# Weight sums of a seven-product MLP: two of four made by adding transfers, and one copy placed ahead of a cast

## The chip, the cores and the metric

The kernel runs on one core of a Trainium2 chip. The metric is the device time of one execution in microseconds, as the median of several runs. The core's engines are TensorE (PE in the profile; its weight loads are PEld), VectorE (DVE), ScalarE (ACT), GpSimd (POOL) and SyncE (SP). Here SP only issues transfers, and POOL issues those transfers that add to what stands at their destination.

## The reference, cut to what matters

The kernel computes one layer of a diffusion backbone in float32 for 512 latent tokens of width 2048. After the two attention mixers comes the channel mixer, a gated MLP of 5632 hidden features, which is the part that the change touches:

```python
def _conv_ffn(h, w_up, conv_w, conv_b, w_down):
    g, u = jnp.split(h @ w_up, 2, axis=-1)
    T = g.shape[1]
    pad = CONV_W // 2
    gp = jnp.pad(g, ((0, 0), (pad, pad), (0, 0)))
    g = sum(gp[:, j:j + T] * conv_w[j] for j in range(CONV_W)) + conv_b
    return (jax.nn.silu(g) * u) @ w_down
...
        h2 = _modulate(_rmsnorm(x, norm2_w[l]), sh2, s2)
        x = x + g2 * _conv_ffn(h2, w_up[l], conv_w[l], conv_b[l], w_down[l])
    return _rmsnorm(x, final_w)
```

## The kernel before, in words

The hidden features are cut into 44 tiles of 128 (`ft` 0 to 43). Each has a gate half `g` and an `u` half, each the sum over the 2048 input features of weight times activation. Tiles 0 to 2 are multiplied plainly (jobs `("n", ...)` and `("u", ...)`). For each of the tiles 3 to 43 the two halves of the outputs (g, u) times the two halves of the input features form a 2 by 2 block of weights, 128x1024 each: `w11`, `w12`, `w21`, `w22`. Against the 2 by 2 block of the activations (two halves of the features, two halves `h0`, `h1` of the tokens) this is a product of two 2 by 2 matrices, done with seven block products instead of eight. They are jobs `("p", ft, k)`, k from 0 to 6. Product 0 takes `w11`, product 1 `w21`, product 4 the sum `t3`, product 5 `w22`, and products 2, 3 and 6 take other sums of weights. For that, sums of the four weight blocks are made for every tile (`weight_sum`), and sums of activation blocks once, ahead of the tiles (`sums`). In the kernel before, all four weight sums of a tile are subtractions on DVE, 128x1024 each: L1534 makes `ws` 1 = w12 - w11 in the job of product 6 of the tile before; L1537 makes `ws` 2 = w22 - `ws` 1 in the job of product 0; L1540 turns w12 into t3 = w22 - w12 in product 1's; L1544 makes `ws` 2 = w21 - `ws` 2 in product 2's.

Every weight operand is split in a high and a low part: ACT casts it to `wh` (`cast`, L1575) and DVE subtracts that from it, giving `wl` (`low`, L1583). `wh` and `wl` have three buffers each, so a cast waits until PE has finished with the operand three jobs back.

PE collects products in three kinds of PSUM tile, `y`, `z` and `x`. Products 0, 2, 4 and 6 add to one and the same `y` tile, and between them ACT copies its state away (`kept`, L1517, to one of two buffers `m`); product 2 may not start before the copy that follows product 0 is done. DVE puts the copies together (`put_together`, L1522 and L1523), the gate goes through ACT (L1491), DVE (L1495, L1497) and ACT (L1502), is multiplied with `u` (`multiply`, L1506) and is split in `ah` and `al` for the down projection.

The down projection of a group of four tiles is eight jobs `("d", c, dp)`, of 24 matmuls each, that lie between the products of the next group. `DOWN_AFTER` puts them into the tiles with ft % 4 = 1 (after products 0, 1, 3, 4, 6) and ft % 4 = 2 (after 0, 2, 3). The tiles with ft % 4 = 3 and 0 have none. ACT scales the outputs of a down block into two buffers `xs` (L1778) and POOL adds them to `x1_d` in HBM with an adding transfer (L1779).

What sets the order: PE, ACT, DVE and SP get their instructions as the code writes them (`manual_schedule`); those of POOL are placed by the framework's scheduler. In each job `strassen(i)` writes the product i on PE, then the weight sum, then the cast for job i+2, then `after(jobs[i - 1])` (the copies and sums that follow the job before), then the low part for job i+2. Each engine works its queue strictly in order.

Loads are issued by SP out of two rings of three buffers of 512 KB: `wr` for w11, the plain tiles' and the down projection's weights, `rb` for the other three blocks of a tile. `Ring.pump` issues a load as soon as the ring's next buffer has no use left (`used`), at that place of SP's queue.

Of the kernel before, what the change touches and what calls it, by code (L numbers as in the profile page):

```python
# [9 lines left out]
F32 = mybir.dt.float32  # L10
# [3 lines left out]
ALU = mybir.AluOpType  # L14
# [3 lines left out]
P = 128  # L18
# [9 lines left out]
NFT = DFF // P  # L28
# [178 lines left out]
def layer_kernel(ctx: ExitStack, tc: tile.TileContext, small, rope, c_row, cc_row, x_t, ctx_t, ada, ada_k,  # L207
                 w_g0, w_f, w_v, w_uqn, w_uqr, w_ukv, w_o, w_up0, w_up, w_dn, out_t):
    nc = tc.nc
    pe, ve, sc, gp = nc.tensor, nc.vector, nc.scalar, nc.gpsimd  # L210
# [6 lines left out]
    n = [0]  # L217

    def nm(s):
        n[0] += 1  # L220
        return f"{s}{n[0]}"
# [39 lines left out]


    sm = ctx.enter_context(tc.tile_pool(name="sm", bufs=1))
    sm.tile([P, 88], F32, name="edge")
# [20 lines left out]
    modx = cst.tile([P, 96], F32, name="modx")  # L285
# [122 lines left out]
    for i, j, view, d in spread:  # L408
        t, o = (cb, ccb)[i], slice(j * 512, j * 512 + 512)
# [357 lines left out]
    for half in range(2):  # L767
# [18 lines left out]
        for t in order:  # L786
            hl = []
# [594 lines left out]
    class Ring:  # L1382

# [62 lines left out]
    def sums(j):  # L1446

        a, c = hf[j], hf[j + 8]
        d1, d2, d3, d4 = c[:, h1], a[:, h0], a[:, h1], c[:, h0]
        b1_, b2_ = db[:, j:j + 1], modx[:, 56 + j:57 + j]  # L1450

        def first():
            t1[j] = a2k(F32R, apb)
            for t in (t3, t2, t4):
                t[j] = spare.pop(0) if spare else b2k(F32R)
            ve.tensor_tensor(d1, c[:, h1], a[:, h1], op=ALU.add)
# [45 lines left out]
        sc.activation(t, t, AF.Silu)  # L1502
        return t

    def multiply(t, u):
        ve.tensor_tensor(t, t, u, op=ALU.mult)  # L1506
# [13 lines left out]
    def put_together(dst, a, b):  # L1520

        ve.tensor_tensor(b, a, b, op=ALU.add)  # L1522
        ve.tensor_tensor(dst, b[:, h0], b[:, h1], op=ALU.add)  # L1523

    def weight_sum(ft, i):

        if ft >= NFT:
            return
        ra, rb = mem["ra"], mem["rb"]
        w12, w21, w22 = (rb.tiles.get((k, ft)) for k in ("w12", "w21", "w22"))  # L1530
        if i in (1, 2):
            sums_[ft, i] = mem["mm"].tile([P, 1024], F32, tag="ws", name=nm("ws"), bufs=2)
        if i == 1:
            ve.tensor_tensor(sums_[ft, 1], w12, ra.tiles["w11", ft], op=ALU.subtract)  # L1534
            ra.used(("w11", ft))
        elif i == 2:
            ve.tensor_tensor(sums_[ft, 2], w22, sums_[ft, 1], op=ALU.subtract)  # L1537
            rb.used(("w22", ft))
        elif i == 3:
            ve.tensor_tensor(w12, w22, w12, op=ALU.subtract)  # L1540
            rb.used(("w12", ft))
            rb.used(("w22", ft))
        else:
            ve.tensor_tensor(sums_[ft, 2], w21, sums_[ft, 2], op=ALU.subtract)  # L1544
            rb.used(("w21", ft))

    def operand(job):

        ra = mem["ra"]
        if job[0] != "p":  # L1550
            return ra.tiles[job], lambda: ra.used(job)
        ft, k = job[1:]
# [4 lines left out]
        key = ({1: "w21", 4: "w12", 5: "w22"}[k], ft)  # L1557
        return mem["rb"].tiles[key], lambda: mem["rb"].used(key)

    def kept_parts(i):  # L1560
# [158 lines left out]
    def third_tile(i):  # L1719
        b, w = jobs[i][1], weights(i)  # L1720
        if b == 0:
            live["s"] = [b_tile(g_, 2) for g_ in "yz"]
        for j in range(8):
            kt = (b // 2) * 8 + j
            classical(live["s"][b % 2], kt, w[j], kt == 0, kt == KT - 1)
        if b == 1:

            mem["hp"].release()
            mem["hr"].release()
            mem["mm"] = tc.alloc_tile_pool(name="mm", bufs=1, side="right", reuse_waits="tile")  # L1730
            mem["rb"] = Ring(mem["mm"], "rb", 3, items_b)
        cast(i + 2)
        if b < 2:
            t = gate_in(b, live["n"][2 * b])
            fill(2 + b)
            low(i + 2)
            silu(convolve(b, live["n"][2 * b], t))
            fill(2 + b)
            hl = multiply(t, live["n"][2 * b + 1])
            fill(1 - b)  # L1740
            acts[b] = finish(t, hl)
        else:
            fill(3)
            low(i + 2)
            weight_sum(3, b - 1)
            fill(5)


# [21 lines left out]
    def after(job):  # L1770

        if job == ("u", 3):
            live[2] = {"g": live["s"][0], "u": live["s"][1], "t": gate_in(2, live["s"][0])}
        elif job[0] == "d":
            for d, po in enumerate(live["po"]):
                dt = job[2] * 2 + d
                x = mem["mm"].tile([P, T], F32, tag="xs", name=nm("xs"), bufs=XS)
                sc.mul(x, po, modx[:, 80 + dt:81 + dt])  # L1778
                gp.dma_start(x1_d[dt], x, accum_op=ALU.add)  # L1779
        if job[0] != "p":  # L1780
            return
        ft, k = job[1:]
        v, f = live[ft], live.get(ft - 1)
        if k == 0:
            v["m1"] = kept(v["y"])
        elif k == 2:
            v["u2"] = kept(v["y"])
            if f:
                silu(convolve(ft - 1, f["g"], f["t"]))
        elif k == 3:  # L1790
            if f:
                acts[ft - 1] = multiply(f["t"], f["u"])
            v["g"] = mem["mm"].tile([P, T], F32, tag="g", name=nm("g"), bufs=1)
            put_together(v["g"][:, h0], v["x"], v["m1"])
            v["m5"] = kept(v["z"])
        elif k == 4:
            if f:
                finish(f["t"], acts[ft - 1])
            v["u"] = mem["mm"].tile([P, T], F32, tag="u", name=nm("u"), bufs=1)
            put_together(v["u"][:, h1], v["y"], v["m5"])  # L1800
        elif k == 5:
            put_together(v["u"][:, h0], v["z"], v["u2"])
        elif k == 6:
            sc.copy(v["g"][:, h1], v["y"][:, h1])
            ve.tensor_tensor(v["g"][:, h1], v["y"][:, h0], v["g"][:, h1], op=ALU.add)
            v["t"] = gate_in(ft, v["g"])

    def strassen(i):
        job = jobs[i]
        if job[0] == "p":  # L1810
            ft, k = job[1:]
            product(ft, k, weights(i))
            if k in (1, 2) or (k == 0 and ft > 3):
                weight_sum(ft, k + 2)
# [12 lines left out]
        low(i + 2)  # L1827


# [209 lines left out]
```

## Time and profile before

| | |
|---|---|
| runs shown, us | 2363.7, 2368.77, 2368.84 (median 2368.77) |
| profiled execution, us | 2363.86 |
| its span, first to last instruction, us | 2362.0 |
| PE busy over the span | 2307.2 us, 98% |
| DVE busy over the span | 1738.1 us, 74% |
| ACT busy over the span | 1141.0 us, 48% |
| POOL busy over the span | 243.6 us, 10% |
| mean granted TensorE clock | 0.994 |
| tiles 3 to 43 with their seven products | from 1052 to about 2300 us of the span |

A busy time counts the modelled length of the instructions. A matmul's end is modelled, and matmuls overlap, so PE can show as busy while it loses time: the distance between the starts of two products tells more than the busy share. In a row of the timeline the bracket at the end is how long the engine sat idle before that row, and what ended it. In rows of waits the numbers are the sum of the idle time, the number of waits, and the longest.

### The profile page before, as it was taken

What the parts mean: (1) busy time and instruction counts of PE and PEld (TensorE: products, weight loads), DVE (VectorE), ACT (ScalarE), POOL (GpSimd) and SP (SyncE); (2) the same over time, 40 slices, a digit from 0 to 9 for tenths busy, and PEclk for the clock granted to TensorE, in tenths of its full rate; (3) what the DMA queues carried; (4) which work ended last, traced back from release to release, by engine and by line L of the source; (5) the groups of instructions that cost most, each with busy time, mean ns of one, the idle gap of its engine ahead of it and who ended that gap; (6) DMA issues with size and microseconds to landing.
All of it is one profiled execution on the core that took longest, in us unless ns stands there. A gap on an engine that the chain in (4) does not pass through costs nothing.

```text
span 2362.0 us, 32374 instructions
## 1 busy us (share of the span) xinstructions
PE 2307.2 (98%) x12526; PEld 1969.4 (83%) x12526; DVE 1738.1 (74%) x2280; ACT 1141.0 (48%) x1736; POOL 243.6 (10%) x258
## 2 busy tenths in 40 slices
PE   6999999999999999999999999999999999999998
PEld 4788888888788888898888888888888888888887
DVE  7998786599977766597585858585857576767767
ACT  5331221477867622364454445454545454544546
POOL 0000000100033213000101010101010101011110
PEclk7999999999999999999999999999999999999999
DMA  9968888635311188334637474646464656455573
GB/s 344 341 256 311 324 341 316 197 119 139 135 60 41 50 329 291 98 106 126 160 105 169 110 169 109 155 128 152 125 141 128 143 141 144 122 156 125 144 188 107
DMA packets 130492, 404.25 MB, mean 171 GB/s; under 512 B 14337, under 2 KB 25089, under 8 KB 119841
## 3 DMA queue, kind: packets, MB, share of 16 engines
q1 hardware_dynamic: 103858, 351.64, 44.8%
q0 software_dynamic: 25328, 49.49, 12.1%
q8 instruction: 98, 1.61, 0.3%
q10 hardware_dynamic: 1152, 1.05, 0.1%
q14 instruction: 56, 0.46, 0.1%
HBM read 332.45 MB, written 69.67 MB: 170 GB/s over the span
## 4 chain that ended last, share of the span: by engine, by line
PE 77%; issue 14%; DVE 4%; ACT 2%; POOL 1%; DMA 1%; SPq 0%; DVEq 0%; POOLq 0%; ACTq 0%
PE y L1758 10%; PE b L258 9%; PE b L259 9%; PE b L260 9%; PE z L1758 5%; PE y L1760 5%; PE s L258 4%; PE s L259 4%; PE s L260 4%; PE s L862 4%; PE z L1760 3%; PE x L1758 2%; PE f L258 2%; PE f L259 2%; PE f L260 2%
## 5 line engine op out<-in xcount | busy, mean ns | idle before, releaser
L1583 DVE TENSOR_TENSOR wl<-wr,wh 128x1024 fp32r<-128x1024 f32 x144 | 176.4, 1225 | 155.1 <-ACT wh L1575 154.3
L1575 ACT CAST wh<-wr 128x1024 fp32r<-128x1024 f32 x144 | 150.9, 1049 | 229.7 <-PE b L259 120.1
L1779 POOL DMA_DIRECT2D x_d<-xs x160 | 139.7, 995 | 1159.4 <-ACT xs L1778 1156.9
L258 PE MATMUL b<-ah,wh 128*128 128x512 f32 (+1 forms) x664 | 256.8, 387 | 0.0
L259 PE MATMUL b<-al,wh 128*128 128x512 f32 (+1 forms) x664 | 256.7, 387 | 0.0
L260 PE MATMUL b<-ah,wl 128*128 128x512 f32 (+1 forms) x664 | 255.9, 385 | 0.0
L1583 DVE TENSOR_TENSOR wl<-rb,wh 128x1024 fp32r<-128x1024 f32 x123 | 150.0, 1220 | 127.1 <-ACT wh L1575 127.1
L1575 ACT CAST wh<-rb 128x1024 fp32r<-128x1024 f32 x123 | 129.3, 1051 | 181.7 <-PE b L259 111.9
L1583 DVE TENSOR_TENSOR wl<-ws,wh 128x1024 fp32r<-128x1024 f32 x123 | 150.1, 1220 | 89.6 <-ACT wh L1575 89.6
L1575 ACT CAST wh<-ws 128x1024 fp32r<-128x1024 f32 x123 | 128.2, 1042 | 131.5 <-PE b L259 45.3
L326 DVE CUSTOM_DVE_ANT_0 ada<-ada,cb,smt 128x2048 f32<-128x2048 f32 x64 | 152.9, 2397 | 36.4 <-DMA ada<-in_ada 36.0
L1758 PE MATMUL y<-a2k,wh 128*128 128x512 f32 x656 | 164.0, 392 | 0.0
L260 PEld LDWEIGHTS b<-ah,wl 128*128 128x128 f32 x664 | 124.8, 188 | 25.8
L234 ACT CAST wh<-wr 128x1024 fp32r<-128x1024 f32 x53 | 55.7, 1052 | 186.8 <-PE b L260 48.4
L258 PEld LDWEIGHTS b<-ah,wh 128*128 128x128 f32 x664 | 125.1, 188 | 22.9
L259 PEld LDWEIGHTS b<-al,wh 128*128 128x128 f32 x664 | 125.1, 188 | 21.9
L258 PE MATMUL b<-a2k,wh 128*128 128x512 f32 (+1 forms) x372 | 138.8, 373 | 2.1 <-DVE n L1656 1.6
L259 PE MATMUL b<-a2k,wh 128*128 128x512 f32 (+1 forms) x372 | 138.1, 371 | 0.1
L260 PE MATMUL b<-a2k,wl 128*128 128x512 f32 (+1 forms) x372 | 137.3, 369 | 0.4 <-DVE wl L235 0.4
L1758 PEld LDWEIGHTS y<-a2k,wh 128*128 128x128 f32 x656 | 118.6, 189 | 21.6
L1758 PE MATMUL y<-b2k,wh 128*128 128x512 f32 x410 | 107.0, 391 | 0.0
L867 ACT ACTIVATE p<-s,m 128x768 f32<-128x768 f32 x96 | 86.8, 905 | 38.7 <-DVE m L865 36.9
(479 smaller groups left out, 5811.0 us busy)
## 6 DMA issues: line engine op xcount, KB each, us to landing
ada<-in_ada SPq DMA_DIRECT2D x80, 1024.0 KB, 7.1
rb<-in_w_up SPq DMA_DIRECT2D x123, 512.0 KB, 4.5
wr<-in_w_dn SPq DMA_DIRECT2D x88, 512.0 KB, 4.0
x_d<-xs POOLq DMA_DIRECT2D x160, 256.0 KB, 6.0
wr<-in_w_up SPq DMA_DIRECT2D x53, 512.0 KB, 4.1
wr<-in_w_f SPq DMA_DIRECT2D x34, 512.0 KB, 7.3
adak<-in_ada_k SPq DMA_DIRECT2D x32, 512.0 KB, 6.4
wr<-in_w_o SPq DMA_DIRECT2D x32, 512.0 KB, 6.4
```

Of the source, the lines that this page charges most:

```text
L234: sc.copy(dst_h, src)
L258: pe.matmul(out, st[0], mv[0], start=start, stop=False, **kw)
L259: pe.matmul(out, st[0], mv[1], start=False, stop=False, **kw)
L260: pe.matmul(out, st[1], mv[0], start=False, stop=stop, **kw)
L326: ve.tensor_tensor_reduce(out=junk, in0=w, in1=vec, op0=ALU.mult, op1=ALU.add, scale=1.0, scalar=col("b_ada", j), accum_out=dst[:, j:j + 1])
L862: pe.matmul(s()[:, c0:c1], a, b[:, c0:c1], start=i == 0, stop=i == len(ms) - 1)
L867: step("ACT", 0.9, t + cost + 1.2, lambda: sc.activation(p(), s()[:, :TT], AF.Exp, bias=m(), accum_out=lcol()), r=[s, m], w=[p, l], lag=0.25)
L1575: sc.copy(t, raw[:, k * n_:k * n_ + n_])
L1583: ve.tensor_tensor(t, raw[:, k * n_:k * n_ + n_], hi[k].bitcast(F32), op=ALU.subtract)
L1758: pe.matmul(o, w[j][0], hs[j], start=start and j == 0, stop=False, skip_group_check=True)
L1760: pe.matmul(o[:, h0], w[j][1], hs[j][:, h0], start=False, stop=j == 7, skip_group_check=True)
L1779: gp.dma_start(x1_d[dt], x, accum_op=ALU.add)
```

## The change

Two of the four weight sums leave DVE. All four are now sums with plus signs: `ws` 1 = w12 + w11, t3 = w12 + w22, `ws` 2 = w22 + `ws` 1, and `ws` 2 = w21 + `ws` 2. The first two are made by transfers: SP loads w12 once into the `ws` buffer (`load_sum`, in the job of product 2 of the tile before) and once into the ring `rb` as `t3`; POOL then adds w11 to the one (`add_first`, written in the job of product 4 of the tile before) and w22 to the other (`add_third`, in product 6's), with transfers that read HBM and add into SBUF. So w12, w11 and w22 are each read twice from HBM. The other two sums stay on DVE as additions. The uses of the ring entries go down accordingly.

The signs are carried by the activations: `db` is a difference, `nb2` is the negative of a column block of `modx`, `sums` forms two of its four differences with a `scalar_tensor_tensor` that multiplies by -1, and `multiply` becomes a `scalar_tensor_tensor` with a sign (-1 for the tiles made by seven products).

Last, in a job that follows a product 0, the copy of that product (`after`) now stands ahead of the cast for job i+2 on ACT.

```diff
     db = sm.tile([P, 8], F32, name="db")
-    ve.tensor_tensor(db, modx[:, 56:64], modx[:, 48:56], op=ALU.add)
+    ve.tensor_tensor(db, modx[:, 56:64], modx[:, 48:56], op=ALU.subtract)
+    nb2 = sm.tile([P, 8], F32, name="nb2")
+    ve.tensor_scalar(out=nb2, in0=modx[:, 56:64], scalar1=-1.0, scalar2=None, op0=ALU.mult)
...
-            items_a.append((("w11", ft), w_up[ft - 2, 0, 0], 2))
+            items_a.append((("w11", ft), w_up[ft - 2, 0, 0], 1))
-            items_b += [(("w12", ft), w_up[ft - 2, 1, 0], 2), (("w21", ft), w_up[ft - 2, 0, 1], 2),
-                        (("w22", ft), w_up[ft - 2, 1, 1], 3)]
+            items_b += [(("t3", ft), w_up[ft - 2, 1, 0], 1), (("w21", ft), w_up[ft - 2, 0, 1], 2),
+                        (("w22", ft), w_up[ft - 2, 1, 1], 2)]
...
-            ve.tensor_tensor(d2, d1, a[:, h0], op=ALU.subtract)
+            ve.scalar_tensor_tensor(out=d2, in0=d1, scalar=-1.0, in1=a[:, h0], op0=ALU.mult, op1=ALU.subtract)
...
-            ve.tensor_tensor(d4, c[:, h0], d2, op=ALU.subtract)
+            ve.scalar_tensor_tensor(out=d4, in0=c[:, h0], scalar=-1.0, in1=d2, op0=ALU.mult, op1=ALU.subtract)
...
-    def multiply(t, u):
-        ve.tensor_tensor(t, t, u, op=ALU.mult)
+    def multiply(t, u, sign=-1.0):
+        ve.scalar_tensor_tensor(out=t, in0=t, scalar=sign, in1=u, op0=ALU.mult, op1=ALU.mult)
...
+    def load_sum(ft):
+        if ft < NFT:
+            sums_[ft, 1] = mem["mm"].tile([P, 1024], F32, tag="ws", name=nm("ws"), bufs=2)
+            nc.sync.dma_start(sums_[ft, 1], w_up[ft - 2, 1, 0])
+    def add_first(ft):
+        if ft < NFT:
+            gp.dma_start(sums_[ft, 1], w_up[ft - 2, 0, 0], accum_op=ALU.add)
+    def add_third(ft):
+        if ft < NFT:
+            gp.dma_start(mem["rb"].tiles["t3", ft], w_up[ft - 2, 1, 1], accum_op=ALU.add)
...
-        if i == 1:
-            ve.tensor_tensor(sums_[ft, 1], w12, ra.tiles["w11", ft], op=ALU.subtract)
-            ra.used(("w11", ft))
-        elif i == 2:
-            ve.tensor_tensor(sums_[ft, 2], w22, sums_[ft, 1], op=ALU.subtract)
-            rb.used(("w22", ft))
-        elif i == 3:
-            ve.tensor_tensor(w12, w22, w12, op=ALU.subtract)
-            rb.used(("w12", ft))
+        if i == 2:
+            sums_[ft, 2] = mem["mm"].tile([P, 1024], F32, tag="ws", name=nm("ws"), bufs=2)
+            ve.tensor_tensor(sums_[ft, 2], rb.tiles["w22", ft], sums_[ft, 1], op=ALU.add)
             rb.used(("w22", ft))
         else:
-            ve.tensor_tensor(sums_[ft, 2], w21, sums_[ft, 2], op=ALU.subtract)
+            ve.tensor_tensor(sums_[ft, 2], rb.tiles["w21", ft], sums_[ft, 2], op=ALU.add)
             rb.used(("w21", ft))
...
+            if k == 2:
+                weight_sum(ft, 4)
+            elif k == 0 and ft > 3:
+                weight_sum(ft, 2)
+            elif k == 4:
+                add_first(ft + 1)
             elif k == 6:
-                weight_sum(ft + 1, 1)
+                add_third(ft + 1)
+            if k == 2:
+                load_sum(ft + 1)
...
-        cast(i + 2)
-        after(jobs[i - 1])
+        if jobs[i - 1][0] == "p" and jobs[i - 1][2] == 0:
+            after(jobs[i - 1])
+            cast(i + 2)
+        else:
+            cast(i + 2)
+            after(jobs[i - 1])
         low(i + 2)
```

The built programs show what this moves. On ACT, in the jobs of products 0 and 1 of tile 8 (ft % 4 = 0), the rows before are these; `wh_11110` is the cast for product 2, `wh_11135` that for product 3, and `m_11138` takes the copy of product 0:

```order
L1575 CAST wh_11110<-ws_11108 128x1024
L1804 COPY g_11033<-y_10906 128x256
L1491 ACTIVATE t_11115<-g_11033,smt 128x512
L1575 CAST wh_11135<-ws_11079 128x1024
L1517 COPY m_11138<-y_11089 128x512
L1575 CAST wh_11158<-rb_10979 128x1024
```

and now, at the same place:

```order
L1582 CAST wh_11119<-ws_11117 128x1024
L1816 COPY g_11043<-y_10914 128x256
L1493 ACTIVATE t_11124<-g_11043,smt 128x512
L1519 COPY m_11143<-y_11098 128x512
L1582 CAST wh_11145<-ws_10982 128x1024
L1582 CAST wh_11168<-rb_10988 128x1024
```

The copy has changed places with one cast of 128x1024; nothing else on ACT has moved there.

On DVE, from the end of tile 7 into tile 8, the rows before are these (L1534, L1537, L1540 and L1544 are the four sums, L1583 the low parts):

```order
L1583 TENSOR_TENSOR wl_11056<-wr_10699,wh_11055 128x1024
L1534 TENSOR_TENSOR ws_11079<-rb_10979,wr_10699 128x1024
L1522 TENSOR_TENSOR m_11002<-z_10907,m_11002 128x512
L1523 TENSOR_TENSOR u_11059<-m_11002 128x256
L1583 TENSOR_TENSOR wl_11084<-rb_10981,wh_11083 128x1024
L1537 TENSOR_TENSOR ws_11108<-rb_11008,ws_11079 128x1024
L1805 TENSOR_TENSOR g_11033<-y_10906,g_11033 128x256
L1583 TENSOR_TENSOR wl_11111<-ws_11108,wh_11110 128x1024
L1540 TENSOR_TENSOR rb_10979<-rb_11008,rb_10979 128x1024
L1583 TENSOR_TENSOR wl_11136<-ws_11079,wh_11135 128x1024
L1544 TENSOR_TENSOR ws_11108<-rb_10981,ws_11108 128x1024
```

and now:

```order
L1590 TENSOR_TENSOR wl_11066<-wr_10705,wh_11065 128x1024
L1524 TENSOR_TENSOR m_11011<-z_10915,m_11011 128x512
L1525 TENSOR_TENSOR u_11069<-m_11011 128x256
L1590 TENSOR_TENSOR wl_11093<-rb_10990,wh_11092 128x1024
L1548 TENSOR_TENSOR ws_11117<-rb_11017,ws_10982 128x1024
L1817 TENSOR_TENSOR g_11043<-y_10914,g_11043 128x256
L1590 TENSOR_TENSOR wl_11120<-ws_11117,wh_11119 128x1024
L1590 TENSOR_TENSOR wl_11146<-ws_10982,wh_11145 128x1024
L1551 TENSOR_TENSOR ws_11117<-rb_10990,ws_11117 128x1024
```

Two of eleven rows are gone, and the order of the others stands.

On POOL, in the second tile with down blocks (ft 6), only the outputs of the down blocks stood before (`x_d_113` to `x_d_118`, two for each block); now the two adding transfers for tile 7 stand among them, `ws_10724` (`add_first`) and `rb_10793` (`add_third`):

```order
L1791 DMA x_d_113<-xs_10698 128x512
L1791 DMA x_d_114<-xs_10701 128x512
L1535 DMA ws_10724<-in_w_up 128x1024
L1539 DMA rb_10793<-in_w_up 128x1024
L1791 DMA x_d_115<-xs_10786 128x512
L1791 DMA x_d_116<-xs_10789 128x512
L1791 DMA x_d_117<-xs_10858 128x512
L1791 DMA x_d_118<-xs_10861 128x512
```

The scheduler has put both ahead of the outputs of the group's last two down blocks, although the code writes `ws_10724` behind the first block's outputs (`x_d_115`, `x_d_116`) and `rb_10793` behind all four.

More of the change, by code (lines that the diff above doesn't have):

```diff
@@ L263, in layer_kernel @@
     sm = ctx.enter_context(tc.tile_pool(name="sm", bufs=1))
-    sm.tile([P, 88], F32, name="edge")
+    sm.tile([P, 80], F32, name="edge")
     rim = ctx.enter_context(tc.tile_pool(name="rim", bufs=1, side="right"))
@@ L1449, in sums @@
         d1, d2, d3, d4 = c[:, h1], a[:, h0], a[:, h1], c[:, h0]
-        b1_, b2_ = db[:, j:j + 1], modx[:, 56 + j:57 + j]
+        b1_, b2_ = db[:, j:j + 1], nb2[:, j:j + 1]
         def first():
@@ L1455, in first @@
                 t[j] = spare.pop(0) if spare else b2k(F32R)
-            ve.tensor_tensor(d1, c[:, h1], a[:, h1], op=ALU.add)
+            ve.tensor_tensor(d1, c[:, h1], a[:, h1], op=ALU.subtract)
         def second():
@@ L1528, in weight_sum @@
             return
[L1529 to L1532, printed above, removed]
-        if i == 1:
-            ve.tensor_tensor(sums_[ft, 1], w12, ra.tiles["w11", ft], op=ALU.subtract)
-            ra.used(("w11", ft))
-        elif i == 2:
-            ve.tensor_tensor(sums_[ft, 2], w22, sums_[ft, 1], op=ALU.subtract)
-            rb.used(("w22", ft))
-        elif i == 3:
-            ve.tensor_tensor(w12, w22, w12, op=ALU.subtract)
-            rb.used(("w12", ft))
+        rb = mem["rb"]
+        if i == 2:
+            sums_[ft, 2] = mem["mm"].tile([P, 1024], F32, tag="ws", name=nm("ws"), bufs=2)
+            ve.tensor_tensor(sums_[ft, 2], rb.tiles["w22", ft], sums_[ft, 1], op=ALU.add)
             rb.used(("w22", ft))
         else:
-            ve.tensor_tensor(sums_[ft, 2], w21, sums_[ft, 2], op=ALU.subtract)
+            ve.tensor_tensor(sums_[ft, 2], rb.tiles["w21", ft], sums_[ft, 2], op=ALU.add)
             rb.used(("w21", ft))
@@ L1556, in operand @@
             return sums_[ft, 1 if k == 3 else 2], None
-        key = ({1: "w21", 4: "w12", 5: "w22"}[k], ft)
+        key = ({1: "w21", 4: "t3", 5: "w22"}[k], ft)
         return mem["rb"].tiles[key], lambda: mem["rb"].used(key)
@@ L1731, in third_tile @@
             mem["rb"] = Ring(mem["mm"], "rb", 3, items_b)
+            load_sum(3)
         cast(i + 2)
@@ L1738, in third_tile @@
             fill(2 + b)
-            hl = multiply(t, live["n"][2 * b + 1])
+            hl = multiply(t, live["n"][2 * b + 1], 1.0)
             fill(1 - b)
@@ L1744, in third_tile @@
             low(i + 2)
-            weight_sum(3, b - 1)
+            if b == 2:
+                add_first(3)
+                add_third(3)
+            else:
+                weight_sum(3, 2)
             fill(5)
@@ L1791, in after @@
             if f:
-                acts[ft - 1] = multiply(f["t"], f["u"])
+                acts[ft - 1] = multiply(f["t"], f["u"], 1.0 if ft == 3 else -1.0)
             v["g"] = mem["mm"].tile([P, T], F32, tag="g", name=nm("g"), bufs=1)
@@ L1824, in strassen @@
             output_block(job[1], weights(i))
-        cast(i + 2)
-        after(jobs[i - 1])
+        if jobs[i - 1][0] == "p" and jobs[i - 1][2] == 0:
+            after(jobs[i - 1])
+            cast(i + 2)
+        else:
+            cast(i + 2)
+            after(jobs[i - 1])
         low(i + 2)
```

2 lines of the change are left out of this document (removed).

## The prediction

> **What bounds the kernel now.** First the busy time of the engines by stretch. The two rows are tiles 15 and 16, which have no down blocks, and then the stretch with down blocks behind them, down to the start of tile 19 (columns: length, then PE, PEld, DVE, ACT and POOL busy, granted clock, DMA share, GB/s).
>
> ```profile
> 1423.70:1463.70 40.00, 39.60 (x226) 34.49 (x225) 36.80 (x45) 22.57 (x29) 0.00 (x0) 1.00 0.33 106
> 1466.50:1546.30 79.80, 79.80 (x402) 67.96 (x401) 45.11 (x50) 37.21 (x50) 13.93 (x16) 1.00 0.66 151
> ```
>
> PE bounds both at full granted clock. DVE is 92% busy without down blocks and 57% with them; the transfers are the other way round, 0.33 and 0.66. So whatever is to be won on DVE lies in the tiles without down blocks, and whatever is put on the transfers weighs in the others. Then what PE waited for from 1050 to 2300 us (sum, number, longest):
>
> ```profile
> PE y L1758 <- ACT m L1517: 6.8, 13, 1.8
> PE z L1758 <- ACT m L1517: 1.1, 1, 1.1
> ```
>
> These are all of its waits, 7.9 us in 14, each for ACT's copy of a product. The timeline of PE shows how one looks (starts of products 0 to 3 of tile 16), and the two long ones in the first tile, 3:
>
> ```profile
> 1443.52 2.00 PE L1758 MATMUL y<-a2k,wh 128*128 128x512 f32 x8
> ...
> 1446.32 2.00 PE L1758 MATMUL x<-a2k,wh 128*128 128x512 f32 x8
> ...
> 1449.65 0.96 PE L1758 MATMUL y<-tp,wh 128*128 128x512 f32 x3 [0.38 <-ACT m L1517]
> ...
> 1452.55 2.00 PE L1758 MATMUL z<-a2k,wh 128*128 128x512 f32 x8
> ...
> 1059.72 0.74 PE L1758 MATMUL y<-tp,wh 128*128 128x512 f32 x2 [1.83 <-ACT m L1517]
> 1069.49 0.73 PE L1758 MATMUL z<-tp,wh 128*128 128x512 f32 x2 [1.12 <-ACT m L1517]
> ```
>
> Product 0 takes 2.80 us from start to start. Product 1 takes 3.33, 0.54 too long, where the row counts 0.38 as idle; and product 2, which starts from a standstill, takes 2.90, 0.10 longer. So one wait costs some 0.26 us more than the waits view says, and all 14 cost 7.9 + 14 x 0.26 = 11.5 us. That is the most that this change can win in the products.
>
> Why the copy is late shows in the rows of ACT and DVE around it:
>
> ```profile
> 1445.55 1.05 ACT L1575 CAST wh<-ws 128x1024 fp32r<-128x1024 f32 x1 [4.48 <-PE y L1758]
> ...
> 1448.09 1.03 ACT L1575 CAST wh<-ws 128x1024 fp32r<-128x1024 f32 x1
> 1449.02 0.57 ACT L1517 COPY m<-y 128x512 f32<-128x512 f32 x1
> ...
> 1440.89 1.22 DVE L1534 TENSOR_TENSOR ws<-rb,wr 128x1024 f32<-128x1024 f32 x1
> ...
> 1444.22 1.22 DVE L1537 TENSOR_TENSOR ws<-rb,ws 128x1024 f32<-128x1024 f32 x1
> ...
> 1448.38 1.22 DVE L1540 TENSOR_TENSOR rb<-rb,rb 128x1024 f32<-128x1024 f32 x1
> 1449.51 1.22 DVE L1583 TENSOR_TENSOR wl<-ws,wh 128x1024 fp32r<-128x1024 f32 x1
> ```
>
> DVE ends L1537 at 1445.44, ACT casts its result from 1445.55, then does the gate, a second cast at 1448.09, and only then the copy that PE waits for. DVE comes late because L1534 stands 1.13 us (start to start, L1540 to L1583) ahead in its queue.
>
> **The change part by part.** *The copy ahead of the cast.* It starts 0.93 us sooner (1448.09 to 1449.02) and PE is 0.54 late, so this alone clears the wait of tile 16. The cast behind it serves product 3, due at 1452.55; ended 0.6 us later, at about 1449.7, it is hidden.
>
> *Two sums off DVE.* L1534 and L1540 go, 2 x 1.13 = 2.26 us of each tile's 20 on DVE. The first brings L1537, and with it the chain to the copy, 1.13 us forward, which would clear the 0.54 again. So for the 12 waits that aren't those of tile 3 I take all: 7.9 - 1.83 - 1.12 = 4.95, and 12 x 0.26 = 3.1, together 8.1 us.
>
> *Tile 3.* Its two waits cost 1.83 + 1.12 + 2 x 0.26 = 3.5 us.
>
> ```profile
> 1058.14 1.04 ACT L1575 CAST wh<-ws 128x1024 fp32r<-128x1024 f32 x1
> 1059.09 0.58 ACT L1517 COPY m<-y 128x512 f32<-128x512 f32 x1
> ...
> 1058.44 1.22 DVE L1540 TENSOR_TENSOR rb<-rb,rb 128x1024 f32<-128x1024 f32 x1
> ...
> 1051.51 1.22 DVE L1537 TENSOR_TENSOR ws<-rb,ws 128x1024 f32<-128x1024 f32 x1
> ...
> 1040.50 0.28 PE L260 MATMUL z<-h,wl 128*128 128x256 f32 x1
> ```
>
> The copy moves up by 0.95, and L1540 (1.13) leaves the DVE queue ahead of the second wait. Against that, `load_sum` of this tile writes where older tiles lay, and may go out only after the matmul at 1040.50, the last that reads them. With a load of 4.5 and an adding transfer of 7.7 us (both below) the sum stands at 1052.7, 1.2 us behind L1537's start. So 0.95 + 1.13 - 1.2 = 0.9 at worst, 3.5 at best; I take 2.4, as DVE has 1.13 us less to do ahead of L1537 and the waits don't all add up.
>
> *What replaces the sums.* Of the transfers from 1100 to 2300 us: queue totals (packets, MB, share of 16 engines), issues (KB each, median us to landing), then all of L1779 on POOL (ns, min/median/max) and their time to landing.
>
> ```profile
> q1 hardware_dynamic: 35569, 125.32, 34.1%
> q0 software_dynamic: 23040, 41.95, 22.2%
> ...
> rb<-in_w_up SPq DMA_DIRECT2D x114, 512.0 KB, 4.5
> ...
> x_d<-xs POOLq DMA_DIRECT2D x160, 256.0 KB, 6.0
> ...
> L1779 POOL DMA_DIRECT2D x_d<-xs x160: 851/862/1236, 1105.7 to 2278.1; - x160
> ...
> DMA to landing us min/median/max: 3.9/6.0/9.2
> ```
>
> q0 holds just the 160 adding transfers: 0.222 x 1200 / 160 = 1.67 us of all engines for 256 KB. For 512 KB into SBUF no row exists. It has as many rows of the tile (128), each twice as long: bounded by 1.67 and 3.33 us, 3.33 taken, since bytes decide for plain loads. Its landing: 3.9 at least, 9.2 + 3.33 = 12.5 at most, 6.0 + 1.67 = 7.7 taken. A plain 512 KB costs 0.341 x 1200 / 125.32 x 0.524 = 1.71 us. The change adds 41 loads and 82 adding transfers, 70 + 137 to 273 us, to 676 us in 1200: the share goes from 56% to 73 to 85%. They bound nothing by the sum; what counts is the landing at two places.
>
> *First place, `ws` 1 of a tile whose predecessor and self have no down blocks* (ft % 4 = 0, ten tiles). `load_sum` waits for the buffer, free after the low part at 1449.51, that is 1450.73. The next L1537 comes a tile of 7 x 2.8 us after the one at 1444.22, at 1463.8. Of these 13.1 us the load takes 4.5 and leaves 8.6 for the adding transfer, against 7.7. DVE may start L1537 some 2.5 us later before product 2 suffers (product 2 was due at 1446.32 + 2.8 = 1449.1, and the sum, 1.22, and the cast, 1.05, go before). So it is hidden up to 11.1 us. Behind L1537 in DVE's queue stand the gate's sum (L1805), on which the copy hangs, and low parts. On POOL only `add_third` stands behind `add_first` here, and t3 is due four products later. On SP the loads of t3, w21 and w22 stand behind `load_sum`, but they wait for DVE instructions that come later than its own (L1544, the low parts of products 4 and 5), so it holds none of them back.
>
> *Second place, POOL's queue in the last down blocks.* There `add_third` stands ahead of the outputs of a down block, and the two `xs` buffers come free when those land. Rows of tile 18 and the start of tile 19, first ACT, then POOL, SP with the landing of the `rb` loads, and PE:
>
> ```profile
> 1540.29 0.69 ACT L1778 ACTIVATE xs<-b,modx 128x512 f32<-128x512 f32 x1 [0.63 <-DMA x_d<-xs]
> 1540.88 1.04 ACT L1575 CAST wh<-wr 128x1024 fp32r<-128x1024 f32 x1
> ...
> 1532.00 1.75 POOL L1779 DMA_DIRECT2D x_d<-xs  x2 [9.57 <-ACT xs L1778]
> ...
> 1526.33 0.42 SPq L1396 DMA_DIRECT2D rb<-in_w_up  x1
> ...
> DMA to landing us min/median/max: 4.3/4.8/5.3
> ...
> 1546.35 0.86 PE L1758 MATMUL y<-a2k,wh 128*128 128x512 f32 x3
> ```
>
> ACT already waits here, 0.63 us, and behind it stands the cast for product 0 of tile 19, which ends at 1541.92 and is due at 1546.35: 4.4 us of slack. The t3 load (issued where the load at 1526.33 is) lands by 1531.6, POOL issues `add_third` in 0.86 (1.72 if its cost doubles) and comes to the outputs at 1532.5 to 1533.4 instead of 1532.00; 1.67 to 3.33 us of adding lie before them, and the extra load of `ws` may delay all by 1.7. The outputs land 2.2 to 6.4 us later; I take 0.5 + 3.33 = 3.8, below the slack, so no stall; at the upper end 2.0 us for each of ten groups.
>
> [...]
>
> *Slower instructions.* `multiply` becomes the kind of instruction that L1495 is (DVE; count, busy us, mean ns, idle before):
>
> ```profile
> L1495 DVE SCALAR_TENSOR_TENSOR t<-g,smt,t 128x511 f32<-128x511 f32 x39 | 29.1, 745 | 0.0
> ...
> L1506 DVE TENSOR_TENSOR t<-t,u 128x512 f32<-128x512 f32 x39 | 26.7, 685 | 0.0
> ```
>
> That is 0.06 us more in each tile, on a DVE that has 2.26 us more room there, and as much for the 16 differences of `sums`, 1 us in all before tile 4; `nb2` is one small instruction. I take nothing.
>
> **Sum.** 8.1 + 2.4 = 10.5 us off 2363.86, the profiled execution's own time: 2353.4. That execution is like the fastest of the runs shown; their median, 2368.77, lies 4.9 above it and two of three runs lie there. I forecast 2355, between the two levels and nearer the profile.
>
> **The rivals.** *The last down blocks stall.* If 512 KB of adding costs more than 3.33, the outputs land later, ACT's cast is late and PE waits at the start of the next tile: ten times what exceeds 4.4 us. From 5.5 us it eats the gain; at 6.7 us of engine time (twice the rate of `x_d`) the delay is 0.5 + 6.7 = 7.2, the stall 2.8, and the time 2353 + 28 = 2381. For it: ACT waits there now and DMA is at 0.66. Against: that it would need twice the price per byte of the nearest row.
>
> *The sums come late.* The adding transfer lands after 11.1 us: ten tiles lose what exceeds it, at the upper bound of 12.5 some 14 us, 2367. For: x_d took up to 9.2, and the three `rb` loads go out in the same microseconds. Against: the 9.2 fell in stretches at 0.66, here it is 0.33 before the change.
>
> *Most is given back* in tile 3 and by small waits for `wl` or `m` elsewhere: 0.9 from tile 3 and half of the others, 5 us, 2359 to 2364. For: PE needs a copy, a cast and a low part per product, and any of them can be the next late one.
>
> **How the numbers follow.** This kernel's runs tell about 0.3%, 7 us, from no change. The forecast (gain of 8 to 12 us): 0.58. Most given back or lost by late sums: 0.20. Down blocks stall: 0.22. The forecast's own range is 2350 to 2361; with the rivals, 2349 to 2378, which leaves the far end of the stall out. A tenth of the second case, the latest sums, counts as slower: faster 0.58, same 0.18, slower 0.24.
>
> **What would show it.** Right: in the profile after, PE's waits for L1517 are gone, DVE is near 82% in tiles without down blocks, the DMA share there is 0.6 to 0.77, product starts are 2.8 apart, and the idle time before the `xs` rows grows without PE waiting at product 0. Wrong: PE waiting for `wh` at product 0 of tiles with ft % 4 = 3 (stalled down blocks), or for `wh` or `wl` from `ws` at product 2 (late sums), or adding transfers of 512 KB landing after more than 11 us.

## The result and the profile after

The changed kernel takes 2392.44 us (median of five runs, 2390.56 to 2400.96), the kernel before 2366.19 (five runs, 2363.49 to 2368.84). The ratio is 1.0118 (95% interval 1.0103 to 1.0132): 26 us slower, where the prediction's sum had 10.5 us less. The profiled execution took 2395.5 us.

The waits from 1050 to 2335 us (engine, line, what it waited for: sum, number, longest) show two kinds of loss:

```profile
ACT xs L1790 <- DMA x_d<-xs: 99.0, 64, 4.8
...
PE y L1770 <- ACT m L1519: 18.8, 10, 1.9
...
PE z L1770 <- ACT m L1519: 5.6, 10, 1.0
...
PE y L1770 <- ACT wh L1582: 0.2, 1, 0.2
```

In the kernel before, the first of these rows read:

```profile
ACT xs L1778 <- DMA x_d<-xs: 4.9, 6, 1.2
```

So ACT stands 99 us at the two `xs` buffers, and PE waits ten times, once for each group of four tiles, for the copy of a product, 1.9 us each. The product is number 2 of the tiles with ft % 4 = 3, right behind the last down blocks. The starts of the products in the two traces give the whole account (from the start of product 0 of tile 3 to the start of product 6 of tile 43, the last product, 1246.9 us before, 1275.0 after):

| where | change, us |
|---|---|
| ten tiles with ft % 4 = 3, with the start of their product 0 | +33.8 |
| of it: start of product 1 to start of product 2 | +18.7 |
| of it: product 2 itself | +9.0 |
| of it: wait of product 5 (in tiles 7, 31, 35, 43) | +4.1 |
| of it: late start of product 0 (0 to 0.4 each) and a rest in tile 27 | +2.0 |
| ten tiles with ft % 4 = 0: the wait at product 2 gone | -6.6 |
| the same tiles: a new wait at product 5 | +3.2 |
| tile 3 | -2.3 |
| sum | +28.1 |

The other 3.8 us of the profiled execution lie ahead of tile 3, at 384 us, in code that the change doesn't touch. This part varies from one execution to the next, for a cause that stays open: in the traces of all kernels below tile 3 starts between 1051.0 and 1063.6 us. So kernels are compared by that stretch of tiles too, beside their medians.

Why product 2 is late shows in the same places of the two kernels. POOL in the changed kernel, at the last two down blocks of the first group (the last down block starts on PE at 1165.98):

```profile
1163.14 0.87 POOL L1535 DMA_DIRECT2D ws<-in_w_up  x1 [7.26 <-DMA ws<-in_w_up]
1166.16 0.87 POOL L1539 DMA_DIRECT2D rb<-in_w_up  x1 [2.15 <-issue]
1166.71 2.12 POOL L1791 DMA_DIRECT2D x_d<-xs  x2
1177.51 0.86 POOL L1791 DMA_DIRECT2D x_d<-xs  x1 [8.69 <-ACT xs L1790]
```

The two outputs behind L1539 (`add_third`), and then the same two in the kernel before (its last down block starts at 1164.26):

```profile
L1791 POOL DMA_DIRECT2D x_d<-xs x2: 1223/1398/1573, 1166.7 to 1167.3; - x2
...
DMA to landing us min/median/max: 9.7/10.1/10.6
```

```profile
L1779 POOL DMA_DIRECT2D x_d<-xs x2: 860/1016/1172, 1163.5 to 1164.0; - x2
...
DMA to landing us min/median/max: 7.0/7.5/8.1
```

Counted from the start of the last down block they are issued 1.5 us later here and take 2.8 and 2.4 us more. Over the ten groups the first lands at 10.7 us instead of 5.7, the second at 12.0 instead of 7.5 (medians; the issue is 1.6 us later, and from issue to landing it takes 3.4 and 3.1 us more). ACT, then DVE between ACT's casts, and then PE in the changed kernel:

```profile
1176.53 0.69 ACT L1790 ACTIVATE xs<-b,modx 128x512 f32<-128x512 f32 x1 [4.01 <-DMA x_d<-xs]
1177.91 0.69 ACT L1790 ACTIVATE xs<-b,modx 128x512 f32<-128x512 f32 x1 [0.69 <-DMA x_d<-xs]
1178.50 1.04 ACT L1582 CAST wh<-wr 128x1024 fp32r<-128x1024 f32 x1
...
1184.24 1.05 ACT L1582 CAST wh<-ws 128x1024 fp32r<-128x1024 f32 x1 [3.75 <-DVE ws L1548]
...
1186.77 0.56 ACT L1519 COPY m<-y 128x512 f32<-128x512 f32 x1
```

```profile
1179.57 1.23 DVE L1590 TENSOR_TENSOR wl<-wr,wh 128x1024 fp32r<-128x1024 f32 x1 [4.01 <-ACT wh L1582]
...
1182.91 1.22 DVE L1548 TENSOR_TENSOR ws<-rb,ws 128x1024 f32<-128x1024 f32 x1
```

```profile
1187.38 0.96 PE L1770 MATMUL y<-tp,wh 128*128 128x512 f32 x3 [1.84 <-ACT m L1519]
```

and ACT in the kernel before:

```profile
1172.83 1.04 ACT L1575 CAST wh<-wr 128x1024 fp32r<-128x1024 f32 x1
...
1179.70 1.05 ACT L1575 CAST wh<-ws 128x1024 fp32r<-128x1024 f32 x1 [4.12 <-DVE ws L1537]
...
1183.17 0.58 ACT L1517 COPY m<-y 128x512 f32<-128x512 f32 x1
```

The cast for product 0 comes 12.52 us after the start of the last down block instead of 8.57: 3.95 late. PE does not miss it there, product 0 starts on time at 1179.80. But behind this cast hangs a chain with hardly a gap: DVE's low part, its sums, L1548, ACT's cast of `ws`, the gate, and the copy that product 2 needs. From cast to copy it takes 8.27 us now and 10.34 before, 2.07 less, as the change had promised (1.13 for one sum, 0.93 for the copy's place). Product 2 had already waited 0.13 there. 3.95 - 2.07 + 0.13 = 2.0 us, and from product 1 to product 2 it takes 4.79 us instead of 2.79.

The stretches without and with down blocks (tiles 15 and 16, then 17 and 18) answer to the first rows of the prediction:

```profile
1431.36:1474.83 43.47, 41.30 (x225) 35.80 (x226) 36.39 (x44) 23.55 (x30) 3.63 (x5) 0.96 0.69 176
1474.83:1557.45 82.62, 82.62 (x418) 70.45 (x417) 40.23 (x45) 38.32 (x52) 17.48 (x20) 1.00 0.77 188
```

With down blocks PE is as fast as before in spite of a DMA share of 0.77 (from product 0 of tile 17 to that of tile 19 it took 82.63 us before). The loss is all in the first row, which also shows a granted clock of 0.96.

### The profile page after: what moved, and what is told of

The parts are those of the page before. It is cut to its first block, busy times and chain, and to the rows that moved or that the text cites. A ratio compares the mean times of both kernels' runs of the same rounds, so it can differ in the third digit from the quotient of the medians.

```text
span 2393.7 us, 32641 instructions
## 1 busy us (share of the span) xinstructions
PE 2320.7 (97%) x12526; PEld 1978.8 (83%) x12526; DVE 1653.8 (69%) x2199; ACT 1146.9 (48%) x1736; POOL 314.5 (13%) x340
## 4 chain that ended last, share of the span: by engine, by line
PE 80%; DVE 7%; DMA 7%; issue 2%; ACT 2%; POOL 0%; SPq 0%; ACTq 0%; DVEq 0%; POOLq 0%
PE b L258 10%; PE b L259 9%; PE b L260 9%; PE y L1770 9%; PE y L1772 5%; PE z L1770 4%; DMA x_d<-xs 4%; PE s L258 4%; PE s L260 4%; PE s L259 4%; PE s L862 4%; PE x L1770 2%; PE z L1772 2%; DVE wl L1590 2%; DMA rb<-in_w_up 2%
## 5 line engine op out<-in xcount | busy, mean ns | idle before, releaser
L1791 POOL DMA_DIRECT2D x_d<-xs x160 | 146.2, 1047 | 497.1 <-ACT xs L1790 494.6
L1582 ACT CAST wh<-rb 128x1024 fp32r<-128x1024 f32 x123 | 129.1, 1050 | 166.7 <-PE b L259 71.3
L1790 ACT ACTIVATE xs<-b,modx 128x512 f32<-128x512 f32 x160 | 105.6, 684 | 100.9 <-DMA x_d<-xs 99.0
L1770 PE MATMUL y<-b2k,wh 128*128 128x512 f32 x410 | 112.2, 405 | 0.0
```

Source lines behind the costliest of these rows:

```text
L1582: sc.copy(t, raw[:, k * n_:k * n_ + n_])
L1770: pe.matmul(o, w[j][0], hs[j], start=start and j == 0, stop=False, skip_group_check=True)
```

## The experiments

Two theories stood at the start. *Queue*: the outputs are late because they stand behind `add_third` in POOL's queue, and that hurts because ACT's two casts stand behind the output scalings. *Traffic*: the extra transfers make everything late, in whatever order. A third, that the copy's new place does harm, was tried beside them. The column of tiles is the stretch of the table above, from the profiled execution.

| kernel | median, us | ratio to before (95%) | tiles, us |
|---|---|---|---|
| before | 2365.15 (29 runs), 2365.42 (23) | | 1246.9 |
| after | 2392.44 | 1.0118 (1.0103 to 1.0132) | 1275.0 |
| e1, POOL in written order | 2357.35 | 0.9973 (0.9961 to 0.9984) | 1236.3 |
| e2, copy alone | 2366.37 | 1.0007 (0.9995 to 1.0019) | 1247.2 |
| e3, sums alone | 2400.54 | 1.0143 (1.0128 to 1.0158) | 1283.2 |
| e4, outputs behind casts | 2356.99 | 0.9962 (0.9949 to 0.9975) | 1236.2 |
| e5, t3 on DVE | 2363.95 | 0.9994 (0.9985 to 1.0004) | 1242.8 |
| e6, plain for adding | 2368.21 | 1.0009 (0.9993 to 1.0024) | 1245.8 |
| e7, e4 with the copy behind | 2353.62 | 0.9952 (0.9938 to 0.9965) | 1235.3 |
| e8, e1 and e4 | 2353.69 | 0.9953 (0.9938 to 0.9967) | 1236.6 |

**POOL in written order (e1).** The scheduler had placed `add_third` ahead of the outputs of the last two down blocks; now POOL follows the code. The second part of the edit writes a table load of ACT, behind the tiles, without its helper.

```diff
     with tc.manual_schedule(engines={mybir.EngineType.PE, mybir.EngineType.Activation, mybir.EngineType.DVE,
-                                     mybir.EngineType.SP}):
+                                     mybir.EngineType.SP, mybir.EngineType.Pool}):
         mem["ra"] = Ring(wp, "wr", 3, items_a)
...
-            exp_ln_tables()
+            sc.preload_act_table_set("natural_log_exp_and_others")
```

> The changed kernel, with POOL's instructions in the order in which the code writes them, so that in a group's last tile the four outputs of the last two down blocks stand ahead of add_third. Theory (queue): the loss comes from the outputs behind add_third; they go out 1.5 us sooner and have no 512 KB adding transfer ahead of them, so they land some 3 to 4.5 us sooner, ACT's two casts come as much sooner, and PE's wait of 1.9 us at product 2 of the ten tiles with ft % 4 = 3 falls to under 0.3; 2355 to 2368 us. Rival (traffic): the outputs land late because of all the extra transfers on the same engines, in whatever order; only the 1.5 us of POOL's time come back, the wait falls to about 0.5, the time to 2372 to 2380. Second rival (clock or anything outside this place): 2388 to 2396, as the changed kernel.

2357.35 us, as the queue theory had it. The outputs land at 5.5 and 7.0 us (before: 5.7 and 7.5), though every extra transfer is still made. The waits of ACT and PE:

```profile
ACT xs L1790 <- DMA x_d<-xs: 4.5, 8, 1.5
...
PE z L1770 <- ACT m L1519: 1.0, 1, 1.0
```

PE's one wait is that of tile 3. The traffic theory fell here: 0.5 us of wait per group and 2372 to 2380 would have been left.

**The copy alone (e2).** The kernel before with only the last part of the change.

```diff
-        cast(i + 2)
-        after(jobs[i - 1])
+        if jobs[i - 1][0] == "p" and jobs[i - 1][2] == 0:
+            after(jobs[i - 1])
+            cast(i + 2)
+        else:
+            cast(i + 2)
+            after(jobs[i - 1])
```

> The kernel before with nothing but the copy of product 0 placed ahead of the cast. If the copy's place wins what the prediction said: the waits at product 2 of the ten tiles with ft % 4 = 0 go (0.66 us each), and 1 to 2 us in tile 3, together 7 to 9 us: 2357 to 2360 against 2366. If the next late thing takes it back (in the changed kernel product 5 of these tiles waits 0.3 us more on average, for the copy of z): 3 to 5 us, 2361 to 2363. If the copy's place itself is what made the changed kernel slow: over 2375.

No gain, which none of the three had said. PE's waits have moved, not gone:

```profile
PE z L1758 <- ACT m L1517: 7.1, 11, 1.9
PE y L1758 <- ACT m L1517: 0.9, 1, 0.9
```

Product 2 of the tiles with ft % 4 = 0 starts on time (6.6 us won) and product 5 of the same tiles waits for the copy of `z` (7.8 us lost, 0.78 for each). In tile 16, where product 5 waits, DVE works from 1449.38 on without a gap, and ACT's copy waits for the last of it:

```profile
1459.94 0.58 ACT L1517 COPY m<-z 128x512 f32<-128x512 f32 x1 [0.49 <-DVE g L1523]
```

With all four sums on it, DVE starts L1523 13.5 us after product 0 starts, as it did before (13.3), whether PE waits at product 2 or not.

**The sums alone (e3).** The changed kernel with the copy where it was.

```diff
-        if jobs[i - 1][0] == "p" and jobs[i - 1][2] == 0:
-            after(jobs[i - 1])
-            cast(i + 2)
-        else:
-            cast(i + 2)
-            after(jobs[i - 1])
+        cast(i + 2)
+        after(jobs[i - 1])
```

> The changed kernel with the copy behind the cast, as before. Theory (queue): the copy stands in the chain that is late behind the last down blocks, so product 2 of the ten tiles with ft % 4 = 3 waits 0.9 us more, 2.8 instead of 1.9, and the time is 7 to 12 us more than the changed kernel's, 2399 to 2405; in tiles with ft % 4 = 0 no wait comes back, since the sum taken off DVE is 1.13 us and the wait was 0.54. If the copy's place was of no use: within 3 us of the changed kernel, 2389 to 2395. If it did harm: under 2389.

2400.54 us, and product 2 behind the last down blocks waits 2.75 us on average (2.9 at most), as the queue theory said. In the tiles with ft % 4 = 0 the sums alone win 5.8 us: product 2 starts 0.07 late on average, and product 5 does not wait.

```profile
PE y L1770 <- ACT m L1519: 28.8, 12, 2.9
```

**Outputs behind the casts (e4).** The changed kernel, with `after` of a group's last down block moved behind the casts for products 0 and 1 of the next tile. POOL's order stays.

```diff
-            after(jobs[i - 1])
+            if jobs[i - 1][0] != "d" or jobs[i - 1][2] != 7:
+                after(jobs[i - 1])
         low(i + 2)
+        if job[0] == "p" and job[2] == 6 and job[1] % 4 == 2 and job[1] > 4:
+            after(("d", job[1] // 4 - 1, 7))
```

> The changed kernel, with the two output scalings of each group's last down block written on ACT behind the casts for products 0 and 1 of the next tile instead of ahead of them. The transfers, their order on POOL and their landing stay. Theory (queue): the late landing hurts only because these two casts, and with them the chain to product 2, stand behind the scalings; PE's waits at product 2 and behind it (33 us in the ten tiles) go, 2356 to 2364 us. Rival (traffic): the extra transfers also make the loads late, the waits stay in part, over 2375.

2356.99 us. The outputs land as late as in the changed kernel (10.8 and 12.1 us), and ACT still waits for them, but nothing hangs on it:

```profile
1176.62 1.05 ACT L1582 CAST wh<-rb 128x1024 fp32r<-128x1024 f32 x1 [1.70 <-PE z L1770]
1177.61 0.69 ACT L1790 ACTIVATE xs<-b,modx 128x512 f32<-128x512 f32 x1
1178.90 0.69 ACT L1790 ACTIVATE xs<-b,modx 128x512 f32<-128x512 f32 x1 [0.59 <-DMA x_d<-xs]
1181.10 1.05 ACT L1582 CAST wh<-ws 128x1024 fp32r<-128x1024 f32 x1 [1.51 <-DVE ws L1548]
```

e1 and e4 each take away one half of the cause, and either is enough.

**t3 back on DVE (e5).** Only `ws` 1 is made by an adding transfer.

```diff
-                        (("w22", ft), w_up[ft - 2, 1, 1], 2)]
+                        (("w22", ft), w_up[ft - 2, 1, 1], 3)]
...
+        elif i == 3:
+            t3_ = rb.tiles["t3", ft]
+            ve.tensor_tensor(t3_, rb.tiles["w22", ft], t3_, op=ALU.add)
+            rb.used(("w22", ft))
...
-                add_third(3)
...
-            elif k == 6:
-                add_third(ft + 1)
+            elif k == 1:
+                weight_sum(ft, 3)
```

> The changed kernel, with only w12 + w11 made by an adding transfer; t3 = w12 + w22 is an addition on DVE again, behind the low part for product 2, and add_third is gone. POOL still has add_first ahead of the outputs of the last down blocks, 3 us sooner than them. Theory (add_third ahead of the outputs is the whole loss): the outputs land no more than 2 us later than before (5.7 and 7.5 us after the last down block's start, against 10.7 and 12.0 in the changed kernel), within the 2 us that the chain to product 2 has won, so that wait is gone; the 1.13 us more on DVE bring back the wait at product 5 in tiles with ft % 4 = 0, between the changed kernel's 0.3 and the copy-alone kernel's 0.8: 2357 to 2364 us. Rival (either adding transfer does it): outputs 3 us later, a wait of about 1 us at product 2 of each of the ten tiles, 2370 to 2380.

2363.95 us, at the upper edge. The outputs land at 6.5 and 8.9 us, so `add_first`, issued 3 us ahead, costs them 0.8 and 1.4; product 2 is 0.03 late. The waits that are left are at product 5, 1.7 us in all in the tiles expected, and 4.2 us in the tiles behind the last down blocks, which was not (e6 shows why):

```profile
PE z L1773 <- ACT m L1519: 5.4, 7, 2.0
```

**Plain transfers in place of adding ones (e6).**

```diff
-            gp.dma_start(sums_[ft, 1], w_up[ft - 2, 0, 0], accum_op=ALU.add)
+            gp.dma_start(sums_[ft, 1], w_up[ft - 2, 0, 0])
...
-            gp.dma_start(mem["rb"].tiles["t3", ft], w_up[ft - 2, 1, 1], accum_op=ALU.add)
+            gp.dma_start(mem["rb"].tiles["t3", ft], w_up[ft - 2, 1, 1])
```

> The changed kernel with both transfers of POOL as plain loads at the same place, so that the weight sums of these two products are left out (only the second block of weights arrives); instructions, order and bytes read stay. If adding has a price of its own (512 KB added held the outputs behind it up by 3.1 to 3.4 us, against the 1.7 us that a plain load of 512 KB takes of all engines): the outputs behind it land 1.5 us sooner, 9.2 and 10.4 us after the last down block's start, the wait at product 2 falls from 1.9 to about 0.4, and the time to 2362 to 2372. If only the place in the queue and the bytes count, and adding costs nothing extra: the landings stay at 10.7 and 12.0, the wait at 1.9, 2388 to 2396.

2368.21 us, inside the first range: adding has a price of its own, and a larger one than expected. The outputs land at 7.6 and 9.8 us, 3.2 and 2.2 sooner than behind an adding transfer. Product 2 is 0.07 late, but product 5 of the tiles behind the last down blocks comes 0.8 us late on average and takes 0.1 longer from its standstill:

```profile
PE z L1770 <- ACT m L1519: 7.4, 11, 1.0
```

So the tightest place of that chain is not product 2 but product 5. What product 5 does not pass on of an output's lateness (the second one's, against the kernel before) is 1.2 to 2.3 us, 1.5 on average, from tile to tile. It is the same for the same tile, within 0.02 us, wherever product 5 waits: here, in tiles 7, 31, 35 and 43 of the changed kernel, and in four tiles of e5, whose unexpected 4.2 us it explains.

**e4 with the copy behind the cast (e7).** This leaves the two adding transfers and takes the copy's new place out.

```diff
-        if jobs[i - 1][0] == "p" and jobs[i - 1][2] == 0:
-            after(jobs[i - 1])
-            cast(i + 2)
-        else:
-            cast(i + 2)
-            if jobs[i - 1][0] != "d" or jobs[i - 1][2] != 7:
-                after(jobs[i - 1])
+        cast(i + 2)
+        if jobs[i - 1][0] != "d" or jobs[i - 1][2] != 7:
+            after(jobs[i - 1])
```

> The kernel of e4 (output scalings behind the two casts) with the copy of product 0 behind the cast again, as in the kernel before: the two sums by adding transfers, without the copy's new place. If the sums taken off DVE win what is won and the copy's place only the tile 3 wait: within 3 us of e4, 2355 to 2360. If the copy's place is worth the 8 us that the prediction took for it together with the sums: 2363 to 2367.

2353.62 us, a little below the range and level with e8; both are faster than the two kernels of this study's question. In the tiles the copy's old place is 0.9 us better than its new one (one profiled execution of each). From 1050 us on PE has one wait left, in tile 3, and in the whole stretch of tiles it is busy 1234.5 of 1235.2 us at full clock:

```profile
PE y L1770 <- ACT m L1519: 0.7, 1, 0.7
```

```profile
1051.80:2287.00 1235.20, 1234.49 (x6497) 1063.47 (x6496) 781.62 (x907) 626.25 (x818) 209.65 (x240) 1.00 0.76 191
```

**Both orders (e8).** e1's and e4's edits together.

> The changed kernel with POOL in written order and with the output scalings of the last down block behind the two casts, both. Theory (queue): each of them alone already clears every wait behind the last down blocks, so both together give what one does, 2354 to 2359. If part of the loss were in the tiles' traffic, it would show as a further gain of some us: under 2352.

2353.69 us, just under the range, and the tiles take 1236.6, as with either. Nothing of the traffic is left to be won back.

## Why the prediction was wrong

*The gain was right in size, and came from one part only.* The prediction took 8.1 + 2.4 = 10.5 us off the tiles. With the loss out of the way they take 10.3 to 11.6 less (e1, e4, e7, e8). But it said that the copy's place alone clears the wait of tile 16, and took the sums as a second reason for the same gain. The copy alone cleared that wait and made another one of about the same size at product 5 (e2); the sums alone won 5.8 us of the 6.6 in these tiles (e3) and all of it in e7. The rival "most is given back by small waits" was true for the copy alone.

*Tile 3.* Taken 2.4, measured 2.3 in the changed kernel, but in part by luck: there the first wait went and the second stayed, 1.0 us. Without the copy's new place (e7) each of the two waits became 1.1 us shorter and the sum is again 2.3, so there the copy's place added nothing.

*The price of the adding transfers.* 3.33 us of all engines were taken, bounded by 1.67 and 3.33, since for plain loads bytes decide. In the trace before they do: q1 took 3.27 us of all engines for a MB from 1100 to 2300 us (34.1% of 1200 us for 125.32 MB, nearly all in loads of 512 KB) and 3.14 from 640 to 700 us (19.9% of 60 us for 3.80 MB, none over 384 KB). The price of the adding ones can be estimated from the queue rows from 1100 to 2300 us of e7, and then those of e6, whose transfers are plain:

```profile
q0 software_dynamic: 33984, 81.80, 40.3%
q1 hardware_dynamic: 41328, 146.29, 35.8%
```

```profile
q1 hardware_dynamic: 41045, 145.27, 36.2%
q0 software_dynamic: 33984, 81.80, 32.1%
```

Less the 160 outputs at 1.67 us, as in the kernel before, 76 transfers of 512 KB took (0.403 x 1200 - 267) / 76 = 2.85 us each when adding and (0.321 x 1200 - 267) / 76 = 1.55 when plain. The landing, taken 7.7, was 8.7 (`add_first`) and 9.5 (`add_third`) in the middle in the changed kernel. A DMA share of 73 to 85% was right (76% by these rows), and so was that it bounds nothing.

*The first place* was hidden, as predicted: DVE waited for the sum in `ws` once, 1.0 us. The room of 2.5 us that the prediction gave L1537 there was read at the cast alone. By the chain to the copy, on which product 2 already waited 0.54, it is 1.13 + 0.93 - 0.54 = 1.5 us.

*The second place is the step that failed.* The prediction let the outputs land 3.8 us later (2.2 to 6.4); the measured 5.0 and 4.5 lie in that range, high because the issue came 1.6 us later where 0.5 was taken. Then it said "below the slack, so no stall", with a slack of 4.4 us between the cast and product 0. For product 0 that slack was about right: with the cast 3 to 5 us late, PE lost 0 to 0.4 us there in each group. But the cast has more users than PE. DVE's queue goes on from its low part to the next sum, and ACT's from that sum to the copy, and in four of the ten tiles (7, 11, 15 and 39) product 2 waited for that copy already. In these four, 2.1 us of the cast's lateness did not reach product 2, which is the 1.13 + 0.93 that the change itself takes out of the chain; both numbers stand in the prediction. In the other six it was 2.2 to 2.9 us, and at product 5 it was 1.2 to 2.3 (e6). With the prediction's own 3.8 this leaves 14 us for the ten groups at product 2 and 23 by product 5, and the forecast would have been some 2367 to 2376. The rival of the stalled down blocks named the place and the transfer, but looked for the sign at product 0 and priced it from the same 4.4: by its formula the measured delay costs 1 to 6 us, and it cost 33.8.

*What follows a standstill* was not priced at all. The ten waits of 2.0 us became 33.8 us because product 5 came late as well in some of the tiles, and in the others product 2 ran at a lower clock (0.62 in tile 11, below).

## What to carry to other kernels

The slack of a late instruction is the smallest one over everything that hangs on it, followed through the other engines' queues to their next meeting with the bound engine, and a wait that exists today tells that this room is zero. A transfer that a scheduler places may come to stand ahead of what the code writes before it, so look at what stands behind it in the same queue: here the same transfers in another order turned a loss of 1.2% into a gain of 0.3%. Where two engines feed each other in a ring, moving one instruction forward may only move the wait (e2); here taking work off the engine without a gap removed it (e3, e7).

## What the runs showed of the hardware

**The clock fell after short standstills.** Product 2 of tiles 7 and 11 of the changed kernel, each from its start to the next product's:

```profile
1187.40:1190.30 2.90, 2.90 (x17) 2.55 (x18) 1.99 (x2) 2.55 (x3) 0.00 (x0) 1.00 0.00 0
1313.23:1317.70 4.47, 4.47 (x17) 3.76 (x17) 3.55 (x4) 2.56 (x3) 0.00 (x0) 0.62 0.24 59
```

Both began after some 1.9 us without a matmul. One ran at full clock; the other at 0.62 in the mean, its matmuls 0.43 us apart instead of 0.23 for about 3.4 us, and lost 1.57 us. Over the ten traces, from tile 3 on, such a stretch followed none of 39 standstills with 0.75 to 1.4 us between the starts of two matmuls, 6 of 13 with 2.0 to 2.25 us, and all 10 with 2.75 us or more (those of e3). The records of the granted clock show where these stretches lie. In the changed kernel and in e3 every lowered stretch of the tiles lasts 3.41 us (one, in e3, twice that) at a clock of 0.50, and within a trace all of them start whole multiples of 3.41 us apart, however the standstills lie: in the changed kernel at 1313.25 us and then 37, 74, 111, 148 and 258 times 3.413 us later. So each trace can be divided into stretches of 3.41 us, laid through these starts. The one ahead of the lowered one of tile 11, and that one itself:

```profile
1309.84:1313.25 3.41, 1.48 (x12) 1.20 (x10) 1.68 (x3) 2.68 (x5) 0.00 (x0) 1.00 0.21 82
1313.25:1316.66 3.41, 3.41 (x8) 2.73 (x9) 2.51 (x3) 1.82 (x2) 0.00 (x0) 0.50 0.15 10
```

The 1.93 us without a matmul all lie in the first of them, whereas the 1.84 us ahead of product 2 of tile 7 fall into two, 1.41 and 0.43. In the two traces 17 of these stretches held 1.74 us or more without a matmul, and 16 of them were followed by a lowered one (why the one ahead of tile 43's product 2 in the changed kernel, with 1.85, was not stays open). None at full clock with 1.41 us or less was. That is what the two traces show; why the clock falls they do not.

**Adding cost 2.85 us of the transfer engines for 512 KB, plain 1.55** (the estimates above from e7's and e6's queue rows), in the same queue with the same bytes (81.80 MB in both rows of q0). What stood behind an adding transfer in POOL's queue landed 3.2 and 2.2 us later than behind a plain one (e6), while transfers of the same size elsewhere in the stretch moved it by nothing that could be measured (in e1 the outputs land at 5.5 and 7.0 us, before at 5.7 and 7.5).
